# A hybrid decoder layer on one core: loads of the delta-net's alpha stage issued a chunk ahead, and six smaller moves

## The chip, the cores and the metric

The kernel runs on one core of one Trainium2 chip. The metric is device time in microseconds of one execution, taken as the median of several runs. The engines are called as in the profile: PE (TensorE), DVE (VectorE), ACT (ScalarE), POOL (GpSimd) and SP (SyncE, which here only issues DMAs).

## The reference

One layer of a decoder trunk, in float32, for two inputs: a prompt of 2048 tokens (with 16 meta tokens ahead of it) and 8 running sequences of 4 new tokens. Model width 1024, feed-forward width 2816. Cut to what matters:

```python
hn = rms_norm(x, norm_mix_pre);  proj = hn @ w_in                    # 1024 -> 4616
u, qkv, z, a, bt, gates = split(proj)
y_s5, h = s5_mix(u, ...)                                             # 32 groups, 64 complex states
br_a = (gelu(y_s5) @ w_s5_glu_a) * sigmoid(gelu(y_s5) @ w_s5_glu_b)
q, k, v = silu(short_conv(qkv));  q, k = l2_norm(q), l2_norm(k)      # 4 heads of 128
o, S = gated_delta(q, k, v, g(a), beta(bt), S0)                      # chunked linear attention
br_b = (rms_norm(o) * silu(z)) @ w_gdn_out
x = x + rms_norm((sigmoid(ga) * br_a + sigmoid(gb) * br_b) @ w_out)
x = x + rms_norm((silu(f @ w_ffn_gate) * (f @ w_ffn_up)) @ w_ffn_down)   # f = rms_norm(x)
```

In the delta part each chunk needs `m = strict_lower(beta * k k^T * decay)` and the inverse of `1 + m`. The outputs are both sets of tokens and all states.

## The kernel before, in words

**Stages.** (1) `p1`: projections from `w_in`, in two halves of two token blocks each (a block is 512 tokens, the first one 560 with meta and sample tokens). (2) `merge`: the products of both branches, block by block. (3) `way_out`: `w_out`, the first residual, the second norm. (4) `gate_up`: gate and up products, one level of a Strassen-like scheme. (5) `down`: the last product, in two token halves and four groups of weights (`KGROUPS`), ending with norm and residual.

**Arithmetic.** Large products are three matmuls each (`mm3`, L159 to L161): every operand is split into a rounded high part and a low part. Weights come by `wload` (L131): one DMA by SP into `wr`, ACT writes the high half, POOL and DVE the low half. The split token features of a block lie in "pages", 16 tiles of 560 columns by two rows (`pages`, L1246), four high and four low for a block.

**Order.** In `p1` the S5 setup, the alphas (decay and M of each chunk, `gdn_alpha`, L573), the inverse of 32x32 blocks (`gdn_beta`), the deltas (`gdn_chunk`, L737) and the S5 groups are generators. `tick` (L779) is called after every four column tiles of a projection, twelve matmuls, and moves each queue of generators on by its rate: features 3, alphas 0.5, S5 0.65 or 0.75, deltas 1.0, or 1.4 once the S5 queue is empty. A generator's `yield` is thus a step in the order of the program. The deltas of a half begin when the alphas' queue is empty. At the end of `p1` what is left is drained with nothing beside it. A planner of the language then reorders within this order by its own estimate of times, gives out the places of tiles, and sets the waits; each engine runs its instructions in the planned order, and SP issues its DMAs in that order too.

**What the change touches.** `gdn_alpha` loads a chunk's keys (`kTa`, L584) and decay row (`E`, L562, in `decay_load`), yields, then DVE and ACT make the decay, PE makes `psk` (L590), DVE makes `Z` and masks it (L606), and SP stores it as M (L607). `kTa`, `E` and `Z` share a ring of three places with the tag `al`. `gdn_chunk` solves the block inverse: `px` (L749) in two groups of four small matmuls, each followed by a DVE copy into `X` (L750). `o_out` (L711) norms a chunk's output, waits two steps, transposes it on PE (`pT`, L732) and stores it. `s5_setup` loads C (`ctl`, L1021) just before its transposes (L1044). `to_features` (L243) transposes token rows through two psum tiles `pt`. In `down_tiles` (L1630) each finished token tile is squared, normed and added to `y_prompt` by an accumulating DMA of POOL (L1669).

Of the kernel before, what the change touches and what calls it, by code (L numbers as in the profile page):

```python
# [7 lines left out]
F32 = mybir.dt.float32  # L8
# [7 lines left out]
P = 128  # L16
# [25 lines left out]
HW = BLK + 2 * SMP  # L42
GW = 348
PAIRS = ((0, 348), (696, 348), (1392, 344))
KGROUPS = ((0, 6), (6, 6), (12, 5), (17, 5))
# [27 lines left out]
class Trunk:  # L73
# [168 lines left out]

    def to_features(self, ys, gain, hi, lo):  # L243

        nc = self.nc
        c0 = ys[0][2]
        w = sum(r for _, r, _ in ys)
        for k0 in range(0, 8, 2):
            ps = self.pt.tile([P, 2, 256], F32, tag="pt", name="pst")
            for kt in (k0, k0 + 1):  # L250
                for y, r, c in ys:
                    nc.tensor.transpose(ps[:, kt - k0, c - c0:c - c0 + r], y[:r, kt * P:(kt + 1) * P],
                                        self.ident[:r, :r])
            for kt in (k0, k0 + 1):
                p = ps[:, kt - k0, :w]
                dh, dl = hi[k0 // 2][:, kt - k0, c0:c0 + w], lo[k0 // 2][:, kt - k0, c0:c0 + w]
                nc.scalar.activation(dh, p, AF.Copy, scale=gain[:, kt:kt + 1])
                nc.vector.scalar_tensor_tensor(dl, p, gain[:, kt:kt + 1], dh.bitcast(F32),
                                               op0=OP.mult, op1=OP.subtract)
            yield  # L260
# [312 lines left out]
    def gdn_alpha(self, b):  # L573

        nc, v = self.nc, self.nc.vector
        ch = self.chunks(b)
        n = len(ch)
        i0 = ch[0][0]
        ssk = self.small.tile([P, 5, H], F32, tag="ssk", bufs=1, name="ssk")
        v.memset(ssk, 1.0)  # L580
        zs = []
        for i, (ci, nt, c0) in enumerate(ch):
            kT = self.gd.tile([P, H, P], F32, tag="al", bufs=3, name="kTa")[:, :, :nt]
            nc.sync.dma_start(kT, ap_of(self.qkv_d, 512 * QW + c0, [[QW, P], [P * QW, H], [1, nt]]))  # L584
            e = self.decay_load(ci, nt, self.gd.tile([P, H, P], F32, tag="al", bufs=3, name="E"))
            yield
            self.decay(e, ci, nt, True)
            ps = self.gp.tile([P, H, P], F32, tag="gp", name="psk")[:nt, :, :nt]
            for h in range(H):
                nc.tensor.matmul(ps[:, h], kT[:, h], kT[:, h], start=True, stop=True)  # L590
            dj = self.gd.tile([P, P], F32, tag="dj", bufs=1, name="dj")[:nt, :nt]
            for h in range(H):
                v.scalar_tensor_tensor(dj, ps[:, h], 1.0, self.ident[:nt, :nt], op0=OP.mult, op1=OP.mult,
                                       accum_out=ssk[:nt, i, h:h + 1])
            z = self.gd.tile([P, H, P], F32, tag="al", bufs=3, name="Z")[:nt, :, :nt]
            v.tensor_mul(z, ps, e)
            rk = self.small.tile([P, H], F32, tag="rk", name="rk")
            rb = self.small.tile([P, H], F32, tag="rb", name="rb")
            self.rsqrt(rk, ssk[:, i], 1.0, 4 * EPS, "k")
            v.tensor_mul(rb, rk, self.beta[:, ci])  # L600
            v.tensor_scalar(self.cv_[:, ci], rb, 0.5, None, op0=OP.mult)
            v.tensor_mul(rb, rb, rk)
            v.scalar_tensor_tensor(self.c1[:, ci], rb, -1.0, self.egc[:, ci], op0=OP.mult, op1=OP.mult)
            msk = self.mlo_s if ci == 0 else self.mlo
            for h in range(H):
                v.scalar_tensor_tensor(z[:, h], z[:, h], rb[:nt, h:h + 1], msk, op0=OP.mult, op1=OP.mult)  # L606
            nc.sync.dma_start(ap_of(self.m_d, ci * MS, [[H * P, nt], [P, H], [1, nt]]), z)  # L607
            yield

    def gdn_beta(self, chunks, v):  # L610
# [100 lines left out]
    def o_out(self, o, qn, lo, hi, col):  # L711
# [15 lines left out]
        yield  # L727
        yield
        pT = self.gp.tile([P, H, P], F32, tag="gp", name="pT")
        w = hi - lo  # L730
# [6 lines left out]
    def gdn_chunk(self, ci, c0):  # L737
# [9 lines left out]
        for a in (0, 64):  # L747
            for h in range(H):
                mm(px[a:a + 32, h, 0:32], M[a + 32:a + 64, h, a:a + 32], V[a + 32:a + 64, h])  # L749
            v.tensor_copy(X[a:a + 32], px[a:a + 32, :, 0:32])  # L750
        vc = self.gdn_v(ci, xv)
# [129 lines left out]
    def s5_setup(self):  # L881
# [117 lines left out]

        nc.sync.dma_start(ld[:16], ap_of(io["s5_D"], 0, [[1, 16], [16, G]]))  # L1000

        rrev = self.c2("s5rr")
# [5 lines left out]
        for hf in range(2):  # L1008
# [5 lines left out]
            for d, nm in ((Br, "s5_B_re"), (Bi, "s5_B_im")):  # L1014
                for sl in (lo, hi):
                    nc.sync.dma_start(d[sl], io[nm].rearrange("o g p c -> p (o g) c")[:, h0:h0 + 16])
            cts = []
            for nm in ("s5_C_re", "s5_C_im"):
                ct = self.c2("ctl")[:, :256].rearrange("p (q k e) -> p q k e", q=2, k=2)
                for k in range(2):  # L1020
                    nc.sync.dma_start(ct[:, :, k], ap_of(io[nm], h0 * 16 * 64, [[64, P], [P * 64, 2], [1, 64]]))  # L1021
                cts.append(ct)
            yield
# [24 lines left out]
            for g0 in range(h0, h0 + 16, 4):  # L1048
# [23 lines left out]
                V2 = f4(self.c2("V2"), 8)  # L1072
                outer(V2, (CR, CI), (R2, R1), "n", 1, 9)
                nc.sync.dma_start(self.wv_d[gs, :, 3].rearrange("g p (t c) -> p g t c", c=16), V2)
                yield
# [169 lines left out]

    def pages(self, n):  # L1246
        new = lambda nm: [self.pg.tile([P, 2, PW], F32R, tag="pg", name=nm) for _ in range(n)]
        return new("pgh"), new("pgl")

    def p2_prep(self, b):  # L1250
# [3 lines left out]

        oh, ol = self.pages(2)
        for h in range(H):
# [6 lines left out]

        sh, sl = self.pages(2)
        for m in range(4):
# [91 lines left out]
    def way_rows(self, r, c):  # L1357
# [8 lines left out]
        v.scalar_tensor_tensor(lo[:, :, :r], raw, 0.25, hi[:, :, :r].bitcast(F32), op0=OP.mult, op1=OP.subtract)  # L1366
        x = self.tm.tile([P, D], F32, tag="tm", name="xr")
        src = self.io["x_prompt"] if c < SEQ else self.io["x_sample"]
# [261 lines left out]
    def down_tiles(self, grp, k0, n, wd, gi, last):  # L1630
        nc, v = self.nc, self.nc.vector
        c0 = grp[0][2]
        w = sum(r for _, r, _ in grp)
# [10 lines left out]
        for a, r, c in grp:  # L1644
            both = wide and gi < last
            rr = 2 * r if both else r
            cl = slice(c - c0, c - c0 + rr)
            for half in range(2):
                cs = slice(BLK * half, BLK * half + BLK)
                ps = self.pm.tile([P, BLK], F32, tag="pm", name="psr")[:rr]  # L1650
                for k, (wh, wl) in enumerate(wd):
                    nc.tensor.matmul(ps, hi[:, k, cl], wh[:, cs], start=k == 0, stop=False)  # L1652
                    nc.tensor.matmul(ps, hi[:, k, cl], wl[:, cs], start=False, stop=both and k == n - 1)  # L1653
                    if not both:
                        nc.tensor.matmul(ps, lo[:, k, c - c0:c - c0 + r], wh[:, cs], start=False, stop=k == n - 1)  # L1655
                if gi == 0:
                    nc.scalar.activation(a[:rr, cs], ps, AF.Copy)
                else:
                    v.tensor_add(a[:rr, cs], a[:rr, cs], ps)
            if wide and gi == last - 1:  # L1660
                t = self.lw.tile([SMP, D], F32, tag="lw", name="lows")
                nc.sync.dma_start(t, a[r:2 * r])
                nc.gpsimd.tensor_add(a[:r], a[:r], t)
            if gi == last:
                rs = self.rstd_of([(a, r, c)], "f")
                v.scalar_tensor_tensor(a[:r], a[:r], rs[:r, 0:1], self.r_fpost[:r], op0=OP.mult, op1=OP.mult)
                dst = (ap_of(self.io["y_prompt"], c * D, [[D, r], [1, D]]) if c < SEQ
                       else ap_of(self.io["y_sample"], 0, [[D, r], [1, D]]))
                nc.gpsimd.dma_start(dst, a[:r], accum_op=OP.add)  # L1669

    def conv_out(self):
# [13 lines left out]
    def run(self):  # L1685
# [16 lines left out]
        with ExitStack() as lo:  # L1702
            self.wr = self.pool("wr", 2, lo)
            self.wp.add(self.pool("wp", 3, lo), 3)
            with ExitStack() as pmx, ExitStack() as pgx:
                self.pg = self.pool("pg", 16, pgx, side="right")
                self.pm.add(self.pool("pm", 3, pmx, space=PSUM), 3)
# [17 lines left out]
            with ExitStack() as ph:  # L1725
                self.hh = self.pool("hh", 2, ph, **kw)
                self.small = self.pool("small2", 2, ph, **kw)
                self.ac = self.pool("ac", 2, ph, **kw)
                self.tm = self.pool("tm2", 3, ph, **kw)
                self.fo = self.pool("fo", 2, ph, **kw)  # L1730
# [20 lines left out]
        with ExitStack() as ph:  # L1751
# [8 lines left out]
            self.wr = self.pool("wr3", 2, ph, side="right", **kw)  # L1760
            self.wp.add(self.pool("wp3", 12, ph, side="right", **kw), 12)
            self.down()
# [72 lines left out]
    def p1_features(self, b):  # L1835

        hi, lo = self.pages(4)
        for grp in self.pairs(self.load_tokens(b, True)):
            self.normed(grp, [t for t, _, _ in grp])
            yield  # L1840
            yield from self.to_features(grp, self.g_mix, hi, lo)
        self.xs[b] = hi, lo
# [130 lines left out]
```

## Time and profile before

| | |
|---|---|
| median of 3 runs | 3237.43 us (3235.34 to 3238.28) |
| the profiled execution | 3230.07 us, its span 3228.3 us |
| granted PE clock, mean | 0.978 |
| PE busy | 3095.1 us |
| DVE busy | 2047.1 us |
| ACT, POOL busy | 1127.2 and 892.9 us |
| moved by DMA | 419.29 MB |

The span is the time from the first to the last instruction of the core. A wait's row names the waiting instruction, who ended the wait, and then the total in us, the number of waits and the longest. A row of a timeline is start, duration, engine (with q: its sequencer, as for an issued DMA), line, operation, out<-in. In the slices the granted clock stands behind the busy times: 1.00 is full speed.

### The profile page before, as it was taken

The numbers are of one execution on the slowest core, as the hardware profiler recorded it, in microseconds if no ns is written. First come the engines' busy times: TensorE is split into PE (matmuls) and PEld (weight loads), VectorE is DVE, ScalarE is ACT, GpSimd is POOL, SyncE is SP. The second block draws the span as 40 slices with busy tenths as digits, with TensorE's granted clock in tenths as the row PEclk, the third lists the DMA queues.
The fourth block names the chain that finished last, engine by engine and source line by source line (L and its number), as shares of the span: only waits on it lengthen the run. The fifth ranks groups of instructions, "written<-read, shape, count | busy, mean of one in ns | idle before, by whom it ended". The sixth has DMA issues, their size and how long they took to land.

```text
span 3228.3 us, 47504 instructions
## 1 busy us (share of the span) xinstructions
PE 3095.1 (96%) x17461; PEld 2719.5 (84%) x17461; DVE 2047.1 (63%) x4674; ACT 1127.2 (35%) x1952; POOL 892.9 (28%) x907
## 2 busy tenths in 40 slices
PE   7998989999999999899999899999999999999998
PEld 6887887877777887888788799999999998887776
DVE  6888864557798645644456777777777773245235
ACT  4642222433333224311244444444444444223211
POOL 1133431113332211300211444434434444121110
PEclk9999998999999999999999999999999999999999
DMA  4335556445556645544555533343323335235214
GB/s 120 122 98 164 137 157 179 116 111 141 158 172 180 169 120 149 173 132 134 162 175 190 171 105 105 105 123 106 105 88 105 105 105 174 83 107 133 88 57 70
DMA packets 460552, 419.29 MB, mean 130 GB/s; under 512 B 112330, under 2 KB 384906, under 8 KB 460320
## 3 DMA queue, kind: packets, MB, share of 16 engines
q1 hardware_dynamic: 450048, 382.18, 40.6%
q0 software_dynamic: 10272, 34.09, 3.8%
q8 instruction: 137, 2.24, 0.3%
q14 instruction: 95, 0.78, 0.1%
HBM read 288.27 MB, written 127.65 MB: 129 GB/s over the span
## 4 chain that ended last, share of the span: by engine, by line
PE 67%; DVE 15%; issue 10%; DMA 5%; ACT 2%; POOL 1%; SPq 0%; POOLq 0%; DVEq 0%; ACTq 0%
PE psf L161 9%; PE psf L159 9%; PE psf L160 9%; PE psr L1652 3%; PE psr L1653 3%; PE psr L1655 2%; PE psg L159 2%; PE psg L161 2%; PE psg L160 2%; DVE cy L391 2%; PE psr L1377 2%; PE psr L1378 2%; PE psr L1380 1%; PE psq L159 1%; PE psq L161 1%
## 5 line engine op out<-in xcount | busy, mean ns | idle before, releaser
L159 PE MATMUL psf<-xh,ah 128*128 128x348 f32 (+1 forms) x1848 | 595.0, 322 | 6.2 <-ACT sn L1546 4.5
L160 PE MATMUL psf<-xl,ah 128*128 128x348 f32 (+1 forms) x1848 | 593.8, 321 | 0.0
L161 PE MATMUL psf<-xh,al 128*128 128x348 f32 (+1 forms) x1848 | 593.5, 321 | 0.0
L146 POOL TENSOR_TENSOR wu<-wr,wu 128x512 fp32r<-128x512 f32 x136 | 218.1, 1606 | 690.0 <-ACT wu L144 664.1
L159 PEld LDWEIGHTS psf<-xh,ah 128*128 128x128 f32 x1848 | 348.3, 188 | 8.0 <-ACT sn L1546 5.4
L161 PEld LDWEIGHTS psf<-xh,al 128*128 128x128 f32 x1848 | 348.4, 189 | 0.2 <-DVE al L1486 0.2
L160 PEld LDWEIGHTS psf<-xl,ah 128*128 128x128 f32 x1848 | 348.4, 189 | 0.0
L159 PE MATMUL psg<-pgh,wu 128*128 128x512 f32 (+2 forms) x800 | 301.2, 377 | 1.2 <-ACT gt L1223 1.2
L1652 PE MATMUL psr<-wu,hh 128*128 128x512 f32 (+2 forms) x748 | 295.9, 396 | 3.9 <-ACT hh L1638 3.9
L1653 PE MATMUL psr<-wu,hh 128*128 128x512 f32 (+2 forms) x748 | 295.8, 395 | 0.0
L161 PE MATMUL psg<-pgh,wu 128*128 128x512 f32 (+2 forms) x800 | 290.3, 363 | 4.0 <-DVE wu L147 4.0
L160 PE MATMUL psg<-pgl,wu 128*128 128x512 f32 (+2 forms) x800 | 289.2, 362 | 0.0
L1655 PE MATMUL psr<-wu,hl 128*128 128x512 f32 x704 | 277.3, 395 | 0.0
L147 DVE TENSOR_TENSOR wu<-wr,wu 128x512 fp32r<-128x512 f32 x136 | 121.0, 891 | 130.7 <-ACT wu L144 127.8
L144 ACT ACTIVATE wu<-wr 128x1024 fp32r<-128x1024 f32 x136 | 142.6, 1054 | 133.8 <-DMA wr<-w_ffn_down 48.8
L159 PE MATMUL psq<-pgh,wu 128*128 128x512 f32 (+2 forms) x480 | 183.1, 381 | 4.6 <-ACT gt L1223 4.0
L161 PEld LDWEIGHTS psg<-pgh,wu 128*128 128x128 f32 x800 | 156.0, 195 | 28.7 <-DVE wu L147 4.2
L159 PEld LDWEIGHTS psg<-pgh,wu 128*128 128x128 f32 x800 | 155.8, 195 | 26.6 <-issue 6.1
L160 PE MATMUL psq<-pgl,wu 128*128 128x512 f32 (+2 forms) x480 | 174.4, 363 | 0.0
L161 PE MATMUL psq<-pgh,wu 128*128 128x512 f32 (+2 forms) x480 | 173.7, 362 | 0.0
L1652 PEld LDWEIGHTS psr<-wu,hh 128*128 128x128 f32 (+2 forms) x748 | 138.8, 186 | 39.8 <-ACT hh L1638 4.2
L160 PEld LDWEIGHTS psg<-pgl,wu 128*128 128x128 f32 x800 | 155.9, 195 | 19.2 <-issue 0.2
(498 smaller groups left out, 6721.3 us busy)
## 6 DMA issues: line engine op xcount, KB each, us to landing
wr<-w_in SPq DMA_DIRECT2D x72, 512.0 KB
araw<-w_ffn_gate SPq DMA_DIRECT2D x31, 1024.0 KB
araw<-w_ffn_up SPq DMA_DIRECT2D x31, 1024.0 KB
wr<-w_ffn_down SPq DMA_DIRECT2D x44, 512.0 KB
zg_d<-gt SPq DMA_DIRECT2D x80, 256.0 KB
h_d<-hm SPq DMA_DIRECT2D x44, 348.0 KB
qkv_d<-cy SPq DMA_DIRECT2D x48, 256.0 KB
hr<-h_d SPq DMA_DIRECT2D x16, 768.0 KB
```

What stands on the lines that cost most here:

```text
L144: nc.scalar.activation(hi[:, :n], raw[:, :n], AF.Copy)
L146: nc.gpsimd.tensor_sub(lo[:, :c], raw[:, :c], hi[:, :c].bitcast(F32))
L147: nc.vector.tensor_sub(lo[:, c:n], raw[:, c:n], hi[:, c:n].bitcast(F32))
L159: t.matmul(ps, wh, xh, start=first, stop=False, **kw)
L160: t.matmul(ps, wh, xl, start=False, stop=False, **kw)
L161: t.matmul(ps, wl, xh, start=False, stop=last, **kw)
L391: nc.vector.scalar_tensor_tensor(yp, raw[:, j:j + np_], w[j], yp, op0=OP.mult, op1=OP.add)
L1377: nc.tensor.matmul(o, hi[:, k, :rr], wh[:, cs], start=i == 0, stop=False)
L1378: nc.tensor.matmul(o, hi[:, k, :rr], wl[:, cs], start=False, stop=wide and i == 7)
L1652: nc.tensor.matmul(ps, hi[:, k, cl], wh[:, cs], start=k == 0, stop=False)
L1653: nc.tensor.matmul(ps, hi[:, k, cl], wl[:, cs], start=False, stop=both and k == n - 1)
L1655: nc.tensor.matmul(ps, lo[:, k, c - c0:c - c0 + r], wh[:, cs], start=False, stop=k == n - 1)
```

## The change

- **Alphas.** The loads of the next chunk are issued at the start of a chunk's step, and the store of a chunk's M is put off to the step after, behind these loads. The ring `al` has five places instead of three, and each call has one more step at its end, for the last store.
- **X.** Both groups of `px` matmuls come first, then both copies.
- **pT.** One more step lies between a chunk's norm and its transposes.
- **C rows.** They are loaded into a `tm` tile: the first half's before `W1`, `W2` are reversed, the second half's in the last group of the first half.
- **First block.** Three of four transposed pairs use the ring `gp` of three psum tiles beside `pt`.
- **Last token tile.** `y_prompt`'s rows are loaded ahead, the square and the product with the gain are done in halves, and the sum is stored by SP in two halves in place of POOL's accumulating DMA.
- **Places.** The pages of a block are one high and one low tile, in one ring of two for even blocks (row pitch 576 in block 0, 512 else) and one for odd blocks; the token rows of `way_out` use three tags in turn; the twelve weight tiles of `down` are two rings of six; the `lw` tile is 1120 wide.

```diff
-    def to_features(self, ys, gain, hi, lo):
+    def to_features(self, ys, gain, hi, lo, wide):
...
-            ps = self.pt.tile([P, 2, 256], F32, tag="pt", name="pst")
+            pool, tag = (self.gp, "gp") if wide and k0 else (self.pt, "pt")
+            ps = pool.tile([P, 2, 256], F32, tag=tag, name="pst")
...
@@ gdn_alpha @@
-        zs = []
+        new = lambda nm: self.gd.tile([P, H, P], F32, tag="al", bufs=5, name=nm)
+        def load(ci, nt, c0):
+            kT = new("kTa")[:, :, :nt]
+            nc.sync.dma_start(kT, ap_of(self.qkv_d, 512 * QW + c0, [[QW, P], [P * QW, H], [1, nt]]))
+            return kT, self.decay_load(ci, nt, new("E"))
+        nxt, store = load(*ch[0]), lambda: None
         for i, (ci, nt, c0) in enumerate(ch):
-            kT = self.gd.tile([P, H, P], F32, tag="al", bufs=3, name="kTa")[:, :, :nt]
-            nc.sync.dma_start(kT, ap_of(self.qkv_d, 512 * QW + c0, [[QW, P], [P * QW, H], [1, nt]]))
-            e = self.decay_load(ci, nt, self.gd.tile([P, H, P], F32, tag="al", bufs=3, name="E"))
+            kT, e = nxt
+            nxt = load(*ch[i + 1]) if i + 1 < n else None
+            store()
             yield
...
-            nc.sync.dma_start(ap_of(self.m_d, ci * MS, [[H * P, nt], [P, H], [1, nt]]), z)
+            store = lambda at=ap_of(self.m_d, ci * MS, [[H * P, nt], [P, H], [1, nt]]), z=z: nc.sync.dma_start(at, z)
             yield
+        store()
+        yield
...
@@ o_out @@
         yield
         yield
+        yield
         pT = self.gp.tile([P, H, P], F32, tag="gp", name="pT")
...
@@ gdn_chunk @@
                 mm(px[a:a + 32, h, 0:32], M[a + 32:a + 64, h, a:a + 32], V[a + 32:a + 64, h])
+        for a in (0, 64):
             v.tensor_copy(X[a:a + 32], px[a:a + 32, :, 0:32])
...
@@ s5_setup @@
+        def rows_c(h0):
+            t = self.tm.tile([P, D], F32, tag="tm", name="ctl")[:, :512].rearrange("p (i q k e) -> p i q k e", i=2, q=2, k=2)
+            for i, nm in enumerate(("s5_C_re", "s5_C_im")):
+                for k in range(2):
+                    nc.sync.dma_start(t[:, i, :, k], ap_of(io[nm], h0 * 16 * 64, [[64, P], [P * 64, 2], [1, 64]]))
+            return [t[:, i] for i in range(2)]
+        nxt = rows_c(0)
...
+            cts = nxt
...
+                if g0 == 12:
+                    nxt = rows_c(16)
...
-    def pages(self, n):
-        new = lambda nm: [self.pg.tile([P, 2, PW], F32R, tag="pg", name=nm) for _ in range(n)]
-        return new("pgh"), new("pgl")
+    def pages(self, b, n):
+        pitch = PITCH if b == 0 else BLK
+        out = []
+        for nm in ("pgh", "pgl"):
+            if n == 4 or nm == "pgh":
+                t = self.pg.tile([P, 8 * (PITCH if b % 2 == 0 else BLK)], F32R, tag=f"pg{b % 2}", bufs=2, name=nm)
+                rows = t[:, :8 * pitch].rearrange("p (k c) -> p k c", k=8)
+                at = 0
+            out.append([rows[:, at + 2 * i:at + 2 * i + 2] for i in range(n)])
+            at += 2 * n
+        return out
...
@@ way_rows @@
-        x = self.tm.tile([P, D], F32, tag="tm", name="xr")
+        n = c // P + 1 if c < SEQ else 0
+        x = self.tm.tile([P, D], F32, tag=f"tm{n % 3}", name="xr")
...
@@ down_tiles @@
+            if gi == last and c + r == SEQ:
+                end = self.down_end(a, r, c)
+                next(end)
...
+                if end:
+                    next(end)
...
-                t = self.lw.tile([SMP, D], F32, tag="lw", name="lows")
+                t = self.lw.tile([SMP, D + 96], F32, tag="lw", name="lows")[:, :D]
...
-            if gi == last:
+            if gi == last and not end:
...
+    def down_end(self, a, r, c):
+        nc, v = self.nc, self.nc.vector
+        rows = lambda cs: ap_of(self.io["y_prompt"], c * D + cs.start, [[D, r], [1, cs.stop - cs.start]])
+        halves = [slice(0, BLK), slice(BLK, D)]
+        y = self.lw.tile([P, D + 96], F32, tag="lw", name="yl")[:, :D]
+        nc.sync.dma_start(y, rows(slice(0, D)))
+        g = self.ac.tile([P, D], F32, tag="ac", name="fg")
+        ss = self.small.tile([P, 2], F32, tag="sse", bufs=1, name="sse")
+        rs = self.small.tile([P, 1], F32, tag="rse", bufs=1, name="rse")
+        yield
+        for i, cs in enumerate(halves):
+            j = self.c2("sq").bitcast(BF16)[:, :BLK]
+            nc.scalar.activation(j, a[:, cs], AF.Square, accum_out=ss[:, i:i + 1])
+            v.tensor_mul(g[:, cs], a[:, cs], self.r_fpost[:, cs])
+            if i == 0:
+                yield
+        v.tensor_add(ss[:, 0:1], ss[:, 0:1], ss[:, 1:2])
+        self.rsqrt(rs, ss[:, 0:1], 1.0 / D, EPS, "e")
+        for cs in halves:
+            v.scalar_tensor_tensor(g[:, cs], g[:, cs], rs[:, 0:1], y[:, cs], op0=OP.mult, op1=OP.add)
+            nc.sync.dma_start(rows(cs), g[:, cs])
+        yield
...
-                self.pg = self.pool("pg", 16, pgx, side="right")
+                self.pg = self.pool("pg", 2, pgx, side="right")
...
-                self.tm = self.pool("tm2", 3, ph, **kw)
+                self.tm = self.pool("tm2", 1, ph, **kw)
...
-            self.wp.add(self.pool("wp3", 12, ph, side="right", **kw), 12)
+            self.wp.add(self.pool("wp3", 6, ph, side="right", **kw), 6)
+            self.wp.add(self.pool("wp5", 6, ph, side="right", **kw), 6)
```

More of the change, by code (lines that the diff above doesn't have):

```diff
@@ L43 @@
 GW = 348
+PITCH = 576
 PAIRS = ((0, 348), (696, 348), (1392, 344))
@@ L594, in gdn_alpha @@
                                        accum_out=ssk[:nt, i, h:h + 1])
-            z = self.gd.tile([P, H, P], F32, tag="al", bufs=3, name="Z")[:nt, :, :nt]
+            z = new("Z")[:nt, :, :nt]
             v.tensor_mul(z, ps, e)
@@ L1016, in s5_setup @@
                     nc.sync.dma_start(d[sl], io[nm].rearrange("o g p c -> p (o g) c")[:, h0:h0 + 16])
[L1017 to L1022, printed above, removed]
+            cts = nxt
             yield
@@ L1253, in p2_prep @@
         width = BLK + SMP if b == 0 else BLK
-        oh, ol = self.pages(2)
+        oh, ol = self.pages(b, 2)
         for h in range(H):
@@ L1262, in p2_prep @@
                        self.g_gdn[:, 0:1])
-        sh, sl = self.pages(2)
+        sh, sl = self.pages(b, 2)
         for m in range(4):
@@ L1631, in down_tiles @@
         nc, v = self.nc, self.nc.vector
+        end = None
         c0 = grp[0][2]
@@ L1835, in p1_features @@
     def p1_features(self, b):
-        hi, lo = self.pages(4)
+        hi, lo = self.pages(b, 4)
         for grp in self.pairs(self.load_tokens(b, True)):
@@ L1840, in p1_features @@
             yield
-            yield from self.to_features(grp, self.g_mix, hi, lo)
+            yield from self.to_features(grp, self.g_mix, hi, lo, b == 0)
         self.xs[b] = hi, lo
```

## The prediction

> **What bounds the kernel now.** I read the page first, then the waits of PE, then busy time in 20 us slices with the granted clock, and last the timelines of the slices that stood out. The page gives the span and the busy shares:
>
> ```profile
> span 3228.3 us, 47504 instructions
> ...
> PE 3095.1 (96%) x17461; PEld 2719.5 (84%) x17461; DVE 2047.1 (63%) x4674; ACT 1127.2 (35%) x1952; POOL 892.9 (28%) x907
> ```
>
> PE does work in 3095.1 of 3228.3 us, so 133.2 us are PE idle, and no part of the change takes a matmul away. The change can only return idle time, or clock. Who ended PE's waits (total, times, longest):
>
> ```profile
> PE pst L252 <- DVE xt L241: 19.1, 3, 13.3
> PE psk L590 <- DMA kTa<-qkv_d: 9.5, 1, 9.5
> PE px L740 <- DVE X L750: 9.1, 7, 3.1
> PE pT L732 <- DVE o L726: 8.7, 4, 6.0
> ...
> PE pst L1044 <- DMA ctl<-s_C_re: 6.0, 2, 4.2
> PE pst L1044 <- DMA ctl<-s_C_im: 5.2, 2, 4.9
> PE pst L252 <- issue: 4.8, 1, 4.8
> ...
> PE pw L1147 <- DVE Z L596: 3.7, 2, 3.3
> ...
> PE pst L252 <- DVE pgl L258: 2.3, 3, 1.1
> ```
>
> All but the first are waits at lines that the diff touches or feeds. They lie in the first two stages (the projections with S5 setup, alphas and deltas beside them). The slices show what goes with them (columns: slice, sum, PE, PEld, DVE, ACT, POOL busy, then the granted clock):
>
> ```profile
> 220.00:240.00 20.00, 15.56 (x84) 13.77 (x84) 13.83 (x64) 3.26 (x6) 10.99 (x13) 0.83 0.43 100
> ...
> 300.00:320.00 20.00, 15.10 (x78) 13.62 (x79) 15.63 (x56) 5.34 (x10) 4.78 (x5) 0.74 0.58 172
> ...
> 360.00:380.00 20.00, 15.80 (x83) 14.04 (x84) 12.51 (x32) 4.38 (x9) 10.70 (x12) 0.83 0.37 110
> ...
> 920.00:940.00 20.00, 16.69 (x65) 13.38 (x65) 19.13 (x77) 4.97 (x10) 6.55 (x12) 0.83 0.67 184
> ...
> 2000.00:2100.00 100.00, 100.00 (x630) 100.00 (x630) 74.56 (x85) 43.90 (x67) 46.10 (x27) 1.00 0.37 113
> ```
>
> A stalled slice loses twice: PE sits idle, and the clock is down (0.74 instead of 1.00 in 300 to 320). In the gate and up stage (2000 to 2100) nothing is idle and the clock is 1.00; the change has nothing to gain there.
>
> **The change part by part.** The sum is made against the profiled execution's own time, 3230.07 us (span 3228.3 and 1.8 around it). That execution lies 7.4 below the median of 3237.43; I carry the difference over.
>
> *C rows and alpha loads (one answer).* SP issues in order, and its timeline shows what stood in front of these loads:
>
> ```profile
> 225.29 0.33 SPq L408 DMA_DIRECT2D qkv_d<-cy  x1
> ...
> 227.15 1.10 SPq L1021 DMA_DIRECT2D ctl<-s_C_re  x2
> ...
> 301.08 0.32 SPq L607 DMA_DIRECT2D m_d<-Z  x1
> ...
> 301.96 0.41 SPq L584 DMA_DIRECT2D kTa<-qkv_d  x1
> ...
> 361.73 0.34 SPq L607 DMA_DIRECT2D m_d<-Z  x1
> 362.12 0.43 SPq L1021 DMA_DIRECT2D ctl<-s_C_im  x1
> ```
>
> The load of kTa at 301.96 stood behind the store of an M (L607), which waits for DVE's last mask; the last C load at 362.12 stood behind the next such store, and the first C loads behind a store of qkv. The change issues a chunk's two loads a whole chunk earlier and ahead of the previous M's store, and asks for the C rows many steps before their transposes. The number of DMAs is the same. What goes from PE: 9.5 (psk), 6.0 + 5.2 (C rows), together 20.7. What goes from the clock, if the three slices went to 1.00: 0.17 + 0.26 + 0.17 of 20 us each, 12.0. Full price 32.7. But DVE has to do the same work in less time, and in those three slices it has 6.2 + 4.4 + 7.5 = 18.1 us free. I take 12, two thirds of that slack, since neighbouring slices are fuller and the next thing late there is DVE's cy for the psum and c2 buffers. Bounds 0 and 32.7.
>
> In the second half of alphas (920 to 940) the same loads free pw (3.7, a psum bank that Z holds) and 0.17 x 20 = 3.4 of clock, but DVE is busy 19.13 of 20 there. Bounds 0 and 7.1; I take 3.
>
> *X copies after both halves of px.* PE's second group of four (rows 64 to 95) waits in the row above for DVE's copy of the first group out of the same tile: 9.1. With both groups ahead of both copies that wait has no cause. The consumer, po, comes a step later. I take 8, bounds 4 and 9.1.
>
> *A step more before pT.* 6.0 of the 8.7 is one wait, of the last chunk, where nothing stands beside it and a step more covers nothing. 2.7 can go; I take 2, bounds 0 and 2.7.
>
> *Four psum tiles instead of two for the first block's transposes.* The wait for pgl (2.3) is a wait for tiles; the issue wait of 4.8 lies in the same block, before the last token tile's transposes, and that tile is loaded into the place of the first. Bounds 0 and 7.1; the xt waits (19.1) are loads and stay. I take 4.
>
> *The last token tile.* The chain behind the last matmul:
>
> ```profile
> 3214.19 0.39 PE L1653 MATMUL psr<-wu,hh 128*128 128x512 f32 x1
> 3214.42 0.40 PE L1655 MATMUL psr<-wu,hl 128*128 128x512 f32 x1
> 3214.86 0.69 DVE L1659 TENSOR_TENSOR facc<-facc,psr 128x512 f32<-128x512 f32 x1 [0.93 <-PE psr L1655]
> 3215.64 1.06 ACT L233 ACTIVATE sq<-facc 128x1024 bf16<-128x1024 f32 x1 [5.82 <-DVE facc L1659]
> ...
> 3216.82 0.15 DVE L102 TENSOR_SCALAR rsx<-ss 128x1 f32<-128x1 f32 x1 [1.27 <-ACT sq L233]
> ...
> 3219.14 1.28 DVE L1666 SCALAR_TENSOR_TENSOR facc<-facc,rs,row 128x1024 f32<-128x1024 f32 x1
> 3220.71 0.86 POOL L1669 DMA_DIRECT2D y_prompt<-facc  x1 [5.64 <-DVE facc L1666]
> ```
>
> From 3214.82 to 3228.3 are 13.5. After: the add 0.7, half a square 0.5 and its read 0.2 with 0.2 of hand-over, one small add 0.2, the root 2.3 (3216.82 to 3219.14), two halves of 0.7 each, an issue of 0.4 and a store by SP. That stands against the page's POOL stores; for SP's 256 KB stores the chain of waits has these two:
>
> ```profile
> 96.27 2.12 DMA zg_d<-gt
> ...
> 982.32 3.87 DMA qkv_d<-cy
> ```
>
> So 0.7 + 0.7 + 0.2 + 0.2 + 2.3 + 1.4 + 0.4 = 5.9, and 2.1 to 3.9 for the store: 8.0 to 9.8. Saved 3.7 to 5.5; I take 4.5. The load of y and the products with the gain lie under the tile's own matmuls.
>
> *Deltas come later.* Each call of the alphas has one step more, two in each half. They step 0.5 per tick, a tick is twelve matmuls of 512 columns at 0.23 us (3214.19 to 3214.42 above), so the deltas of the second half start 4 ticks, 11 us, later. Their end is uncovered already: products of the next stage begin at 1281.08, and chunks 15 and 16 end behind that.
>
> ```profile
> 1144.00 0.36 SPq L735 DMA_DIRECT2D on_d<-oT  x1
> ...
> 1254.23 0.37 SPq L735 DMA_DIRECT2D on_d<-oT  x1
> ...
> 1315.61 0.37 SPq L735 DMA_DIRECT2D on_d<-oT  x1
> ...
> 1331.16 0.36 SPq L735 DMA_DIRECT2D on_d<-oT  x1
> ```
>
> ```profile
> 1281.08 0.30 PE L159 MATMUL psgb<-pgh,wu 128*128 128x272 f32 x1
> ```
>
> A chunk takes 27.6 us under cover (the first two rows are four chunks apart) and 15.6 without (the last two are neighbours). 11 of 27.6 is 0.4 of a chunk; at 15.6 each that is 6.2, part of it filled with products. I take +4; bounds 0 and 15.6 (a whole chunk).
>
> *Pages in one tile each, a row pitch of 576 or 512, tiles tm0 to tm2, two rings of six weights, lw of 1120.* They issue the same instructions on the same sizes. The cover is that pages of one block are written while another block's matmuls run; if a whole page waits where a quarter did, its release comes at most one unit later. Zero, and I count it into the spread of 10 that a re-planned order can bring on either side.
>
> Sum: -12 - 3 - 8 - 2 - 4 - 4.5 + 4 = -29.5. 3230.07 - 29.5 = 3200.6; with the 7.4 between that execution and the median, **3208**.
>
> **The rivals.** *DVE becomes the bound.* For it: 19.13 of 20 busy at 920, and small DVE instructions are stretched in this stage:
>
> ```profile
> 294.69 2.54 DVE L103 TENSOR_SCALAR rsi<-rsx 128x4 int32<-128x4 int32 x1
> ```
>
> The small one at 3216.82 took 0.15. If DVE has no slack to give, the terms of 12 and 3 are nothing and the rest is -14.5: 3223. Against it: 18.1 us of slack in the very slices that stall. The Trainium skill (Advanced Engine Details and Errata, VectorE Performance Modes) says that VectorE's second port is shared with GpSimd and that each can block the other; by that rule POOL's outer products would lengthen DVE's work as they are pushed closer together, which leads to this rival's 3223. No row here tells the port from a plain wait.
>
> *SP waits for the M just stored (slower).* The ring of five gives a load of E the place that an M two chunks back held, so at the head of SP that load waits until the store has landed, and weights, qkv and gates queue behind it. Price: up to 3.87 a chunk (the longer store above). From eight of the 17 chunks on it eats the 29.5; if twelve are exposed, 46.4 - 29.5 = +16.9: 3254. Against it: the store was issued a step before, and weights have a lead:
>
> ```profile
> 875.00 0.38 SPq L142 DMA_DIRECT2D wr<-w_in  x1
> ...
> 891.63 0.39 SPq L142 DMA_DIRECT2D wr<-w_in  x1
> ```
>
> They come every 16.6 us, four times the wait.
>
> *The loads don't move.* The planner orders by its own estimate and may leave SP's order near what it is; then -8 (px) and -4.5 (end) stand against a whole chunk uncovered, +15.6: +3, 3240, no change.
>
> **How the numbers follow.** Forecast 0.68 (its own range 3188 to 3223), DVE bound 0.15, SP waits 0.09, loads don't move 0.08. A measurement of this kernel tells about 0.2% (6.5 us) from no change. The first two are faster, less 0.02 for their edges: 0.81; the third is 0.09 with an edge: same 0.09, slower 0.10. Low end: all bounds at once give -7.1 - 32.7 - 7.1 - 9.1 - 2.7 - 5.5 = -64.2; I stop at 3184, since they hardly come together. High end 3238: the DVE case with a whole chunk uncovered (-2.9) and a few us of a poorer order.
>
> **What would show it.** Right: no wait of psk for kTa, none of L1044's transposes for C rows, px's waits gone, slices 220 to 380 with PE near 20 and the clock at 1.00, DVE above 18 there; the last psr to the end in 8 to 10 us; the last on_d store about 4 us later against the first psgb than the 50.1 here (1281.08 to 1331.16). Wrong: PE waits for cy or wu from DVE where it waited for loads; SP's waits for m_d before an E load; more than 60 us from psgb to the last on_d store; or new stalls in the stages after 1340, where I expect none.

## The result, and the profile after

The changed kernel takes 3193.9 us (median of four, 3191.03 to 3205.06) against 3236.4 us before: a ratio of 0.9875, interval 0.9849 to 0.99, or 42.5 us less. Timed again later beside the kernel before, it took 3194.9 us, ratio 0.9879 (0.9866 to 0.9893). The forecast was 3208 us, 29.5 less; its range (3184 to 3238) holds the time. The sum behind it does not hold: its terms were wrong on both sides.

The page of the profiled execution (3191.03 us), its span and busy times:

```profile
span 3189.3 us, 47489 instructions
...
PE 3064.2 (96%) x17461; PEld 2715.6 (85%) x17461; DVE 2039.3 (64%) x4678; ACT 1129.0 (35%) x1956; POOL 891.9 (28%) x906
```

The span fell by 39.0 us. PE's idle time (span less busy) went from 133.2 to 125.1 us, only 8.1 less. PE's busy time fell from 3095.1 to 3064.2, by 30.9, with the same 17461 matmuls. The prediction was an account of idle time and clock. The time lost to the clock (the sum of one minus the granted share, over the span) went from 70.8 to 65.4 us, so idle time and clock together gave 13.5 of the 39.0 us; some 25 us, most of the gain, are elsewhere. PE's waits after (who ended them, total, times, longest):

```profile
PE pst L254 <- DVE xt L242: 19.6, 4, 13.4
PE pT L742 <- DVE o L735: 10.0, 4, 5.8
PE psk L597 <- DMA kTa<-qkv_d: 7.2, 1, 7.2
PE psq L160 <- ACT gt L1238: 7.0, 4, 4.1
PE psg L160 <- ACT raw L380: 6.5, 3, 5.6
...
PE pw L1162 <- DVE Z L603: 6.0, 2, 3.8
PE psg L160 <- ACT gt L1238: 5.3, 3, 4.4
PE pT L742 <- DVE carry L384: 3.6, 1, 3.6
```

The waits for the C rows (11.2 us before) and of px for X (9.1) have no row any more. The wait for kTa is still there, and waits for ACT's evictions (gt, raw), for Z and for pT have grown. The slices, in the columns of the prediction:

```profile
220.00:240.00 20.00, 13.15 (x84) 11.63 (x82) 12.19 (x56) 3.72 (x9) 9.92 (x13) 0.94 0.47 106
300.00:320.00 20.00, 14.84 (x83) 13.60 (x84) 13.39 (x47) 7.47 (x14) 7.28 (x7) 0.83 0.59 159
360.00:380.00 20.00, 19.19 (x112) 16.42 (x111) 14.98 (x33) 5.15 (x10) 12.12 (x14) 1.00 0.44 121
380.00:400.00 20.00, 15.12 (x82) 13.46 (x81) 19.44 (x33) 5.67 (x12) 12.67 (x11) 0.83 0.43 126
```

Slice 360 is repaired, but slice 380, which stood like this before, has lost what it gained:

```profile
380.00:400.00 20.00, 18.81 (x126) 17.00 (x125) 19.86 (x33) 6.16 (x12) 10.28 (x10) 1.00 0.38 107
```

The end of the kernel is as forecast. Its timeline:

```profile
3180.40 0.69 DVE L1689 TENSOR_TENSOR facc<-facc,psr 128x512 f32<-128x512 f32 x1 [0.23 <-PE psr L1685]
...
3181.93 0.16 DVE L1720 TENSOR_TENSOR sse<-sse 128x1 f32<-128x1 f32 x1
...
3184.44 1.42 DVE L1723 SCALAR_TENSOR_TENSOR fg<-fg,rse,yl 128x512 f32<-128x512 f32 x2
3185.22 1.01 SPq L1724 DMA_DIRECT2D y_prompt<-fg  x2
```

From PE's end at 3180.4 to the end of the span are 8.9 us, in place of 13.5.

**Where the busy time went.** The same matmul starts its follower sooner. The stretches below lie in the down stage, psr alone; a row is the stretch, its length, PE busy, in brackets the number of matmuls that touch it (one or two more than fit), the clock, the DMA share, GB/s. First the kernel before:

```profile
2710.00:2770.00 60.00, 60.00 (x260) 1.00 0.37 119
```

and after:

```profile
2690.00:2750.00 60.00, 60.00 (x266) 1.00 0.33 104
```

No idle time and full clock in both, and yet 266 against 260. Over the whole down stage the mean from the start of one matmul to the start of the next is 232.3 ns before and 226.9 after (2200 pairs each). The operands, shapes and instructions are the same; only places differ. In the kernel before, the stationary rows (hh, hl) lay 128 bytes beyond the moving rows (wu) modulo 512 in the program's layout of SBUF (no trace holds addresses); lw of 1120 instead of 1024 columns moves hh and hl by 96 columns of 4 bytes, and 128 + 384 is 512. Likewise a page row of 560 columns steps by 2240 bytes, 192 more than a multiple of 512, while 512 columns are 2048 bytes and 576 are 2304, a multiple of 256.

### The profile page after: what moved, and what is told of

It is laid out like the page before. It is cut to its first block, busy times and chain, and to the rows that moved or that the text cites. A ratio compares the mean times of both kernels' runs of the same rounds, so it can differ in the third digit from the quotient of the medians.

```text
span 3189.3 us, 47489 instructions
## 1 busy us (share of the span) xinstructions
PE 3064.2 (96%) x17461; PEld 2715.6 (85%) x17461; DVE 2039.3 (64%) x4678; ACT 1129.0 (35%) x1956; POOL 891.9 (28%) x906
## 4 chain that ended last, share of the span: by engine, by line
PE 74%; DVE 14%; DMA 5%; issue 3%; ACT 2%; SPq 1%; POOL 1%; DVEq 0%; ACTq 0%; POOLq 0%
PE psf L162 9%; PE psf L160 9%; PE psf L161 9%; PE psr L1682 5%; PE psr L1683 5%; PE psr L1685 5%; PE psg L160 2%; PE psg L162 2%; PE psg L161 2%; DVE cy L393 2%; PE psr L1403 2%; PE psr L1404 2%; PE psr L1406 1%; PE psgb L161 1%; PE psgb L162 1%
## 5 line engine op out<-in xcount | busy, mean ns | idle before, releaser
L160 PE MATMUL psg<-pgh,wu 128*128 128x512 f32 (+2 forms) x800 | 297.3, 372 | 11.9 <-ACT raw L380 6.5
L1682 PE MATMUL psr<-wu,hh 128*128 128x512 f32 (+2 forms) x748 | 292.0, 390 | 1.8 <-ACT hh L1665 1.8
L1683 PE MATMUL psr<-wu,hh 128*128 128x512 f32 (+2 forms) x748 | 291.9, 390 | 0.0
L162 PE MATMUL psg<-pgh,wu 128*128 128x512 f32 (+2 forms) x800 | 287.0, 359 | 3.2 <-DVE wu L148 3.2
L1512 POOL TENSOR_TENSOR al<-R,ah 128x1024 fp32r<-128x1024 f32 x62 | 161.7, 2609 | 35.5 <-ACT ah L1511 31.6
```

The source lines that it names most:

```text
L160: t.matmul(ps, wh, xh, start=first, stop=False, **kw)
L162: t.matmul(ps, wl, xh, start=False, stop=last, **kw)
L1512: eng.tensor_sub(flat(lo), x, flat(hi).bitcast(F32))
```

## The experiments

Two theories. **A, places:** the distance of moving and stationary rows sets the pace of a matmul. **B, waits:** the prediction's own; the gain is waits that were taken away. The times below are medians; each comes with its ratio to the kernel before on the same chip (3234.8 to 3235.9 us).

### The places alone

```diff
-        new = lambda nm: [self.pg.tile([P, 2, PW], F32R, tag="pg", name=nm) for _ in range(n)]
+                t = self.pg.tile([P, 8 * (PITCH if b % 2 == 0 else BLK)], F32R, tag=f"pg{b % 2}", bufs=2, name=nm)
...
-                t = self.lw.tile([SMP, D], F32, tag="lw", name="lows")
+                t = self.lw.tile([SMP, D + 96], F32, tag="lw", name="lows")[:, :D]
```

> The kernel before with the places alone: pages in one tile each with a row pitch of 576 or 512, the token rows' three tags, two rings of six weights, the lw tile of 1120; every load, step and copy stays as before. Theory A (places set the pace): a 512-column matmul whose moving row and stationary row lie a multiple of 512 bytes apart starts its follower after 227 to 228 ns, others after 230 to 232. Then about 2200 matmuls of the down stage gain 5.5 ns (12 us) and about 3450 of the first two stages 2.6 ns (9 us): 21 us faster than before, about 3215, with the down stage (2699.7 to 3214.8 before) 12 us shorter and no wait of PE gone. Theory B (the prediction's: waits taken away): nothing, within 6 us of before, at most 10 of a re-planned order.

3201.2 us, ratio 0.9896 (0.9883 to 0.991): 33.6 us less. Theory B falls for the larger part of the gain. PE's busy time falls from 3095.1 to 3073.3, 21.8 us, which is what A had worked out; as a whole the kernel is 14 us faster than A's 3215. Its waits are those of before. A stretch of the merge stage, before:

```profile
1520.00:1580.00 60.00, 60.00 (x260) 1.00 0.44 142
```

and with the places alone:

```profile
1520.00:1580.00 60.00, 60.00 (x266) 1.00 0.48 154
```

The profiled execution of this kernel was its slowest of four (3206.5), 23.5 below that of before; the 10 us between that and the medians' 33.6 are not seen in a trace and stay unexplained. So the pace accounts for 22 of the 33.6; the rest is open.

### The steps alone

The changed kernel with the old pages, the one ring of twelve weights, the one ring of token rows and lw of 1024.

> The changed kernel with the old places: pages as 16 tiles of 560 columns by two rows, one ring of three token rows, one ring of twelve weights, the lw tile 1024 wide; the loads ahead, the later stores, the copies of X, the extra step, the psum tiles and the last token tile stay changed. Theory A: what is left without the places is about 18 of the 39 us, so about 3215 to 3220, and the mean start-to-start of 512-column matmuls is back at 231 ns. Theory B: 29.5 or more below before, 3205 or less, next to the changed kernel.

3221.7 us, ratio 0.9962 (0.9948 to 0.9975): 13.1 less. Theory B's 3205 or less falls; A's 3215 to 3220 is just missed. All that the prediction counted is worth 13 us here and not 29.5. With the 33.6 of the places that makes 46.7, against 42.5 measured for both.

### One number: lw

```diff
-                t = self.lw.tile([SMP, D + 96], F32, tag="lw", name="lows")[:, :D]
+                t = self.lw.tile([SMP, D], F32, tag="lw", name="lows")[:, :D]
...
-        y = self.lw.tile([P, D + 96], F32, tag="lw", name="yl")[:, :D]
+        y = self.lw.tile([P, D], F32, tag="lw", name="yl")[:, :D]
```

> The changed kernel with the lw tile 1024 instead of 1120 wide, which moves the stationary rows of the down stage by 384 bytes and nothing else. Theory A: psr of down is back from 227 to 232 ns start to start, the down stage 12 us longer, the whole 12 us slower than the changed kernel (about 3206), all else alike. Theory B: no difference from the changed kernel beyond 0.2%.

3207.5 us, ratio 0.9914 (0.99 to 0.9927), 12.6 to 13.6 more than the changed kernel; psr of down is back at 232.3 ns from start to start, all other groups of 512 columns stay. A holds, to its number.

### Eight distances in one run

```diff
-        hi = self.hh.tile([P, 6, 256], F32R, tag="hh", name="hh")
+        place = lambda nm: self.hh.tile([P, 6 * 256 + 128], F32R, tag=nm, name=nm)[:, off:off + 6 * 256].rearrange("p (k c) -> p k c", k=6)
+        hi = place("hh")
...
-                    self.down_tiles(grp, k0, n, wd, gi, last)
+                    self.down_tiles(grp, k0, n, wd, gi, last, 16 * (4 * half + gi))
```

> The changed kernel with the stationary rows of the down stage shifted by another 64 bytes from one group of weights to the next (0, 64, ... 448 over the eight passes), all else alike. Theory A: the pace of psr follows the distance of moving and stationary rows modulo 512 bytes, as the matmuls of the kernel before suggest: 227 to 228 ns at 0, about 230.5 at 64, 192, 256 and 320, 232 at 128, 384 and 448; as a whole 7 to 8 us slower than the changed kernel. Rival C (the pace goes with the stage, its engines' traffic or the place as such, not with the distance): one pace, 227 ns, in all eight passes.

3197.4 us in a single execution; the 8 us that A expects of the whole are inside the spread of such. One stretch of 40 us from each of the eight passes, in order, so with the stationary rows shifted by 0, 64, 128, ... 448 bytes:

```profile
2690.00:2730.00 40.00, 40.00 (x178) 1.00 0.29 94
2755.00:2795.00 40.00, 40.00 (x173) 1.00 0.20 61
2815.00:2855.00 40.00, 40.00 (x174) 1.00 0.31 99
2870.00:2910.00 40.00, 40.00 (x177) 1.00 0.66 144
2935.00:2975.00 40.00, 40.00 (x179) 1.00 0.30 82
3005.00:3045.00 40.00, 40.00 (x173) 1.00 0.20 61
3070.00:3110.00 40.00, 40.00 (x173) 1.00 0.22 61
3135.00:3175.00 40.00, 40.00 (x176) 1.00 0.46 76
```

The means from start to start are 226.9, 233.3, 232.4, 228.9 and then again 226.9, 233.3, 232.1, 229.1 ns. Rival C (one pace) falls. The period is 256 bytes, not the 512 of theory A, whose 230.5 at 64 and 192 bytes was off too; 128 bytes gives the 232.3 of the kernel before. The sweep moves the stationary rows alone. In the merge stage the change moves the moving rows (the pages) alone, from four mixed distances to one, and the mean there goes from 231.5 to 226.8 ns, so it isn't the place of one operand by itself.

### Equal places in gate and up

```diff
-            hi = pool.tile([P, 4, GW], F32R, tag=nm + "h", bufs=1, name="xh")[:, :, :w]
+            row = 384 if nm in ('t1', 't2', 't3', 't4', 'b22') else GW
+            hi = pool.tile([P, 4, row], F32R, tag=nm + "h", bufs=1, name="xh")[:, :, :w]
...
-            t = self.gt.tile([P, GW], F32, tag="sn", bufs=6, name="sn")[:, :w]
+            t = self.gt.tile([P, GW], F32, tag="sn", bufs=4, name="sn")[:, :w]
```

> The changed kernel with equal places in gate and up as well: the rows of t1, t2, t3, t4 and b22 get a pitch of 384 columns (1536 bytes, three times 512) instead of 348, on the same distance from the stationary rows; to make room, sn has four places instead of six, su two instead of three, th one instead of two. Theory A (places set the pace): 3960 of the 5544 matmuls go from 159 and 157 ns to 348 and 344 columns at 227/512 ns, 154.3 and 152.5, 4.5 ns each: 18 us faster than the changed kernel, about 3176, less what waits for the fewer places cost; the matmuls with b11 and b21 stay as they are. Rival C (the pace goes with the stage or the shape): 159 and 157 ns stay, no gain, and waits for the fewer places show as a loss.

3200.1 us, ratio 0.9893 (0.9879 to 0.9906): 5 to 6 us slower than the changed kernel, which is inside the intervals; the 18 us that A wanted are not there. Before:

```profile
2000.00:2060.00 60.00, 60.00 (x379) 1.00 0.36 112
```

and with equal places:

```profile
2000.00:2060.00 60.00, 60.00 (x381) 1.00 0.30 95
```

The matmuls with equal places went from 159.1 to 158.4 ns at 348 columns and from 156.8 to 157.8 at 344. So the rule of the distance holds for this kernel's 512 columns and doesn't carry over to its 348; what sets the pace there is open. One wait for the fewer su places alone was 7.2 us.

### Without the loads ahead

The changed kernel with kTa, E and Z in three places, the store of M and the loads of C as before, and no extra step of the alphas.

> The changed kernel with the loads of the alphas, the store of M and the loads of C as they were before (three places, no extra step of the alphas); all else changed. The prediction's terms: 12 + 3 us of waits and clock come back, less some 3 of the 4 for later deltas: about 12 us slower than the changed kernel, 3206. Theory G (the waits only moved: TensorE's idle time is 116 us with and 118 without): the waits for C and kTa come back, those for gt and raw at 234, 256 and 381 go, idle time within 6 us of the changed kernel; the time the same, or up to 10 us faster where the deltas start earlier.

3183.1 us, ratio 0.9839 (0.9826 to 0.9852): 10.8 to 11.8 us faster than the changed kernel. The waits for the C rows (6.4 + 5.6) and for kTa (9.8 of 10.9) are back, those for raw (6.5 to 0.5) and gt (12.3 to 5.3) are nearly gone, and idle time is 126.3 us against 125.1. That is theory G: the waits had only moved. Why the kernel is even faster is seen at the end of the first stage. Two stretches (columns as in the slices), before:

```profile
400.00:640.00 240.00, 227.14 (x1529) 194.12 (x1528) 133.12 (x357) 63.54 (x156) 55.56 (x71) 0.93 0.56 151
1240.00:1340.00 100.00, 88.16 (x653) 77.64 (x653) 62.30 (x171) 40.36 (x93) 19.08 (x25) 0.91 0.53 138
```

the changed kernel:

```profile
400.00:640.00 240.00, 231.86 (x1601) 198.79 (x1600) 143.12 (x412) 76.96 (x189) 52.60 (x68) 0.97 0.60 155
1240.00:1340.00 100.00, 83.33 (x639) 76.26 (x638) 60.86 (x155) 39.39 (x84) 22.66 (x27) 0.81 0.45 129
```

and without the loads ahead:

```profile
400.00:640.00 240.00, 229.51 (x1558) 196.68 (x1557) 139.25 (x395) 74.67 (x183) 52.93 (x68) 0.94 0.58 154
1240.00:1340.00 100.00, 89.82 (x701) 83.43 (x700) 72.59 (x168) 43.83 (x87) 30.49 (x32) 0.95 0.64 179
```

In the second stretch the deltas are drained. Idle time and lost clock (one minus the granted share, times the length) together are 11.8 + 9 before, 16.7 + 19 = 35.7 in the changed kernel, 10.2 + 5 = 15.2 here: 20.5 us are lost there by the loads with their steps. In the first they gain 8.1 + 7.2 = 15.3 against 10.5 + 14.4 = 24.9, so 9.6 us. The balance of the two is 10.9. The medians differ by 10.8, but the two profiled executions by 5.2 (3191.0 and 3185.8): other stretches differ by up to 3.3 us either way, so the two stretches are the larger part and not a full account. Why 400 to 640 runs better with later deltas was not tried. The steps alone, above, have the same loss in the drain (78.43 busy at 0.80), so it isn't the places.

### Without the extra steps, and with one call

Three kernels. The first takes the extra steps alone away and keeps the loads ahead:

```diff
             yield
         store()
-        yield
...
         yield
         yield
-        yield
         pT = self.gp.tile([P, H, P], F32, tag="gp", name="pT")
```

> The changed kernel without its extra steps: the last M of a call is stored without a step of its own, and two steps instead of three lie ahead of pT. Theory F (the later deltas cost more than the 4 us of the prediction): the drain of the first stage, 1240 to 1340, where the changed kernel has TensorE busy 83.3 of 100 us at a clock of 0.81 and the kernel before 88.2 at 0.91, comes back to about the latter, and the time falls by 8 to 14 us, to about 3180 to 3186. The prediction's price: 4 us less, 3190, or 2 us of waits for pT back.

3185.7 us, ratio 0.9848 (0.9834 to 0.9861): 8.2 to 9.2 less, F's price and twice the prediction's. The drain (columns as in the slices):

```profile
1240.00:1340.00 100.00, 88.71 (x724) 81.71 (x724) 71.50 (x166) 43.73 (x89) 29.25 (x31) 0.97 0.63 175
```

It loses 11.3 + 3 = 14.3 us here, with the loads still ahead, against 35.7; so the steps cost the drain, and not the loads. The wait for kTa grows to 9.1 us, so it isn't that one that matters.

The second puts both blocks of a half in one call, so that the loads run ahead across the border:

```diff
-        for b in (2 * p, 2 * p + 1):
-            yield from self.gdn_alpha(b)
-            ch += self.chunks(b)
+        ch = self.chunks(2 * p) + self.chunks(2 * p + 1)
+        yield from self.gdn_alpha(ch)
```

> The changed kernel with the alphas of both blocks of a half in one call, so that the loads run ahead across the border of the blocks too, and with one extra step a half instead of two. The wait of psk for kTa (7.2 us at 298 in the changed kernel, 9.5 before) is that of the second block's first chunk, whose load has nothing ahead of which to be issued. Theory D (the loads ahead don't reach that chunk): the wait goes, and with half of a clock stretch of 6.8 us and half the extra steps the time falls by 7 to 12 us, to about 3183 to 3187. Rival E (VectorE and what it waits for from GpSimd set the pace there): the wait goes and another of the same size takes its place between 290 and 400; no difference beyond 0.2%.

3179.8 us, ratio 0.9833 (0.9819 to 0.9846): 14 to 15 less. The wait of psk for kTa has no row left, as theory D said, and E's same time falls, though new waits for gt of 1.9 to 2.4 us at 300, 325, 380 and 390 are E's in kind. The gain is larger than D's 7 to 12, and most of it isn't D's: from 200 to 400, where the wait was, idle time and lost clock went from 39.6 to 34.1, and in the drain, with one extra step less, from 35.7 to 11.7.

The third takes the last step of that call away as well:

> The changed kernel with the alphas of a half in one call and without the extra step at its end, so that the deltas begin when they did in the kernel before. Theory F (each extra step of the alphas, 2 ticks of delay for the deltas, costs about 4 us in the drain): one step less than the run with one call alone (3179.8), whose drain (1240 to 1340) has 8.7 us of idle time and 6.8 us at half clock already; 0 to 4 us faster, 3176 to 3180. Rival E: the drain is at its floor with one step, the same time within 0.2%.

```profile
span 3175.5 us, 47484 instructions
...
PE 3053.5 (96%) x17461; PEld 2704.4 (85%) x17461; DVE 2048.9 (65%) x4676; ACT 1128.2 (36%) x1956; POOL 897.1 (28%) x906
```

3177.2 us, ratio 0.9817 (0.9803 to 0.983). On the same chip the changed kernel took 3194.9 (0.9879): 17.7 us less, and the fastest of all these kernels. The 2.6 us to the run before are within the intervals, and its drain loses 13.2 where that of the run before lost 11.7: with one call a half, one extra step has no price that shows, so E's floor stands against F's 4 us a step.

> The changed kernel as it is, beside the two others on the same chip. If the loads ahead with their steps cost time (3183.1 without them against 3193.9 with them, whose intervals touch): 3190 to 3196, 8 to 14 us slower than the two others. If the difference was one of chips or of disturbed runs: within 0.2% of them.

This is that second timing of the changed kernel. The difference to the runs without the loads ahead is none of chips.

### The third step ahead of pT

> The run without the loads ahead, with two steps instead of three ahead of pT besides: what stays of the change is the places, the copies of X, the psum tiles and the last token tile. The prediction's term: the third step takes 2 us of waits for pT away, so this is 2 us slower than the run without loads ahead (3183.1): 3185. Theory F: a step less ahead of pT shortens the chain of the last chunk too: the same or 2 us faster.

3186.3 us, ratio 0.985 (0.9837 to 0.9864), against 3183.1 with the step: 3.2 us, the sign and about the size of the prediction's 2, but inside the intervals of the two.

This run differs from the one without the extra steps (3185.7) by the loads, the C rows and the store of M alone, which are as before here and ahead there. That is 0.6 us, well inside the intervals: without the steps, loading ahead is worth nothing.

## Why the prediction was right, and where it was not

The runs price the parts in groups: places -33.6; X copies, psum tiles and last token tile together 3186.3 - 3201.2 = -14.9; the third step -3.2; loads, C rows, late store and the alphas' steps 3193.9 - 3183.1 = +10.8. That sums to -40.9, measured -42.5. The prediction had 0, -16.5, -2 and -11. Two errors, of 34 us one way and 22 the other, leave a total that is off by 13; that they offset each other is luck.

**The step that failed first: places at zero.** The prediction said that they "issue the same instructions on the same sizes" and looked for a cost in release times. Its own number, 0.23 us for a matmul of 512 columns, was taken as fixed; 2.4 ns on some 2600 matmuls of the projections, 4.7 on 860 of merge and 5.4 on 2200 of down, some 22 us together, were the largest term. The Trainium skill (TensorE: Matmul & The Clock Gate, Step-by-step: what each phase is for) says that loading the next tile's weights takes no read bandwidth from the running matmul, since PE has two read ports. The sweep doesn't agree as far as time goes: 226.9 or 233.3 ns by nothing but where the stationary rows lie. That the two reads meet in SBUF would fit, but no run here shows it.

**The -12 and -3 for C rows and alpha loads.** The C waits went as forecast, but 15 us did not come of it: with the steps in, the group costs 10.8, and without them loading ahead is worth nothing (3185.7 against 3186.3). The 9.5 of psk did not go (7.2 stay), since the row was misread. SP's timeline of the changed kernel:

```profile
297.60 0.32 SPq L614 DMA_DIRECT2D m_d<-Z  x1
...
301.17 0.44 SPq L586 DMA_DIRECT2D kTa<-qkv_d  x1
```

The load at 301 (301.96 before) is the sixth: the first chunk of the second block, in a call of its own that begins only when the first call has stored its last M. "A whole chunk earlier" holds within a call; at its border nothing is ahead. The run with one call shows it.

**What took the place of the waits.** In the same stretch of the changed kernel, by engine:

```profile
235.64 1.21 POOL L1071 TENSOR_TENSOR ow<-s5c,s5r 128x576 f32<-128x576 f32 x1
236.81 1.26 POOL L147 TENSOR_TENSOR wu<-wr,wu 128x512 fp32r<-128x512 f32 x1
236.89 1.80 DVE L1075 TENSOR_TENSOR V<-V,ow 128x576 f32<-128x576 f32 x1 [5.28 <-POOL ow L1071]
...
238.92 0.63 ACT L573 ACTIVATE E<-E 128x512 f32<-128x512 f32 x1 [15.78 <-DVE E L571]
239.46 0.65 ACT L380 ACTIVATE raw<-psq 128x256 f32<-128x256 f32 x2
```

PE waited 5.6 us at 234 for raw, ACT's eviction of psq. ACT, whose order has the exponential of E ahead of raw, stood at E; E stood on DVE behind V; V waited for POOL's ow. The likely reading is that the C rows came in time and brought the S5 setup and the decay onto one another. This is the rival that had DVE become the bound, with POOL behind it; as a time (3223) it fell, in part because the places were not in it. The rule that the prediction cited for it (the Trainium skill, Advanced Engine Details and Errata, VectorE Performance Modes) is about VectorE's two-port instructions, and the table there gives tensor_tensor no such mode. Yet one more row shows a tensor_tensor that depends on POOL:

```profile
289.80 0.75 DVE L1075 TENSOR_TENSOR V<-V,ow 128x576 f32<-128x576 f32 x1
```

The same operation takes 0.75 us there and 1.80 above, where POOL's subtraction begins 0.08 us ahead of it. The trace of the changed kernel has it eight times: the five that begin with no POOL instruction running take 0.74 to 0.75 us, and the three that begin 0.07 to 0.08 us into one take 1.65 to 1.80 and end 0.61 to 0.62 after that one's end. So these three stood until POOL's instruction had ended, within their own time and beside any wait ahead of them, for which the prediction had no row; that it is the port is not shown. The kernel before has two such rows of eight, and DVE's busy time fell from 2047.1 to 2039.3, so this is not what the steps cost.

**The +4 for later deltas.** Too small: the pairs above make the alphas' steps +10.8 to +11.4, inside the bounds of 0 and 15.6; the drain alone lost 14.9 us against before (35.7 to 20.8). The prediction's mark for "wrong" was more than 60 us from the first psgb to the last store of on_d, in the changed kernel's rows (first and last start):

```profile
L160 PE MATMUL psgb<-pgh,wu x76: 283/290/575, 1244.4 to 1399.8; 128*128 128x272 f32 x64, 128*128 128x512 f32 x12
...
L745 SPq DMA_DIRECT2D on_d<-oT x5: 360/367/371, 1206.6 to 1317.3; - x5
```

It is 72.9, against 50.1 before. Both ends come earlier than before, the first product by 36.7 us and the last store by 13.9: products are taken into the uncovered time, and do not fill it. Without the alphas' steps, in the fastest kernel, it is 43.7:

```profile
L160 PE MATMUL psgb<-pgh,wu x83: 284/290/574, 1257.8 to 1400.0; 128*128 128x272 f32 x64, 128*128 128x512 f32 x19
...
L743 SPq DMA_DIRECT2D on_d<-oT x5: 359/367/371, 1200.7 to 1301.5; - x5
```

The prediction priced a delay of 0.4 chunk by PE's time for a chunk; what it costs besides is the clock, 0.81 over 100 us, in which PE stood still nine times for 0.3 to 5.8 us.

**Right.** Of the signs of being right, the C waits and px's are gone, while slices at full clock with DVE above 18 came at 360 in part only (DVE 14.98). The end: 8.9 us, forecast 8.0 to 9.8. X: no wait of px for X is left. X, psum tiles and the end together: -14.9 against -16.5. The psum tiles' own 4 can't be told apart; before 200 us the idle time fell from 24.7 to 23.1. No stalls of note came up after 1340. None of SP's waits ahead of a load of E or kTa was ended by a store of M (the longest total, 2.6 us in eight, by PE's pn), so the slower rival fell; "the loads don't move" fell too, as the second kTa load moved from 233.06 to 174.18.

## What to carry to other kernels

Before a layout change is costed at zero, count matmuls per stretch without idle time: two stages with the same shape and another pace (512 columns in the kernel before: 227.3 ns in way_out, 232.3 in down) are a sign that places may matter, and the distance of moving and stationary rows is worth a sweep in the stage itself, for what held at 512 columns did not at 348. A wait that goes from one list is a gain only if the whole stretch is shorter; extra steps in a chain whose end is uncovered can be paid at that end, in clock as well as in idle time (two in each half cost some 11 us here, one in the kernel with one call nothing that shows). Loads that are moved ahead must be followed across the borders of calls and loops: there lies the one load that has nothing to be ahead of.

## What the runs showed of the hardware

Matmuls of 512 columns (float32 operands, each with its own load of 128 by 128 stationary values) started every 226.9 ns where the stationary rows lay a multiple of 256 bytes from the moving ones, and every 233.3, 232.4 and 229 ns at 64, 128 and 192 bytes beyond, at full clock and without idle time; both halves of 512 bytes gave the same four paces. At 348 columns an equal distance gave 158.4 ns against 159.1 over all distances, at 344 columns 157.8 against 156.8. The drain at 0.81 granted clock lost 19 us of 100 beside 16.7 us of idle time: in this row of stalls of 0.3 to 5.8 us the clock cost as much as the stalls. A tensor_tensor of DVE (128x576, float32) took 0.74 to 0.75 us, and 1.65 to 1.80 where it began while a POOL instruction ran.
